# Memory rows, cached keys, spatial weights, conv taps, biases and norm weights are laid out feature-major by the host and loaded that way, in place of transposes on TensorE

## The chip, the cores and the metric

The kernel runs as one program on one core of a Trainium2 chip. The metric is the device time of one execution in microseconds (us). Five engines work in parallel, each through its own instructions in order: PE (TensorE, matmuls; its weight loads are shown apart as PEld), DVE (VectorE), ACT (ScalarE), POOL (GpSimd) and SP (SyncE, which here issues most of the loads). They wait for each other and for DMA through semaphores. SBUF is the on-chip memory, PSUM the memory that PE writes.

## What is computed

One layer of a decoder trunk for 256 prompt tokens and 8 sample tokens of one step each, in float32 with model width 2048. With `xn = rmsnorm(x)`:

```python
z = xn @ w_in                                  # 2048 x 9216, split into u, v, q, k, v, memory q, gates
o_g = gelu(zu) * (tril(ws) @ rmsnorm(gelu(zv)) + bs)      # 8 groups of a 128 x 128 matrix
o_a = sliding_window_attention(q, k, v, cached k and v of the samples)
o_m = attention(zm, memory k and v)             # 256 memory rows, 4 heads of 128
x = x + (sig(g0)*(o_g @ w_br_g) + sig(g1)*(o_a @ w_br_a) + sig(g2)*(o_m @ w_br_m)) @ w_out
h = rmsnorm(x) @ w_up                           # 2048 x 11264, then a causal conv of 3 taps + bias
x = x + (gelu(a) * b) @ w_down;  y = rmsnorm(x)
mkv = rmsnorm(mem_prompt) @ w_mem_kv            # 256 rows of 2048 -> 1024: memory k and v of the prompt
```

The conv's weights are `conv_w` (3 taps) and `conv_b` for 11264 channels, the spatial weights `gmlp_ws` and `gmlp_bs`, the norm weights four vectors of 2048, the cached keys 8 x 128 rows x 4 heads of 64. The host may lay inputs out anew before the launch; that is not in the time.

## The kernel before

**Matmuls.** Features lie on the partitions, tokens on the free axis. Each float32 product is made of three float32r matmuls: every operand is split into a high and a low part (`hi` a cast, `lo` the rest), and hi*hi, hi*lo and lo*hi are summed in PSUM. Weights come in **chunks** of 256 rows x 512 or 384 columns (512 or 384 KB). For each chunk SP issues one load into a tile `raw` (4 buffers), ACT casts its two halves to `whi`, DVE takes the rest to `wlo`, and PE runs the chunk's matmuls.

**What sets the order.** `run()` walks over all chunks. Before it emits the matmuls of a chunk it emits the load and the split of the chunk two further on. The class `InOrder` pins every engine to the order in which the code emits. All that is no weight work (norms, attention, transposes, stores, small loads) is put into numbered slots: `at(slot, fn)` and `later(n, fn)` keep a function for the n-th `pump()` from now, and the matmul code calls `pump()` once for every 128 output columns of a chunk (four times for a chunk of 512). So a small load stands on SP's queue between the weight loads of the chunks around it, and when its buffer isn't free, all loads behind it wait too.

**Stages.** The chunks are numbered from 0: q (0 to 15), k and v (16 to 23), memory q (24 to 31, `gemm` with `pre_m`), memory keys and values (32 to 47, `mem_chunk`), u and v of the gating branch (48 to 79), gates and branches, `w_out`, the conv feed-forward, and the final norm. Step k of the memory stage (k = 0 to 7) is chunks 32+2k (keys) and 33+2k (values). It needs rows 256k to 256k+255 of the memory's features: `mem_prep(k)` makes from them `mhi` (ACT) and `mlo` (DVE), two buffers each; it is called at the start of step k-1, behind the split of chunk 32+2k.

**What the change touches.** `mem_load` loads 512 columns of the memory rows for two steps as `ml` (2 buffers, 4 loads), `mem_prep` turns them with four transposes on PE into PSUM (`mtp`), and after the second step ACT takes squares of `ml` for the norm (`junk`, `ssm`). `swa_plan` loads the samples' cached keys as `k`, one per sample, turns each with two transposes (`ktrans`, `kctp`) and copies it to `KT` (`kcopy`, 4 buffers); `kscore` makes four samples' scores `ssp` from it, once for samples 0 to 3 and once for 4 to 7. `conv_plan` turns the taps (`crow`, `ctp`) into `cvT`, `gmlp_plan` the spatial weights (`wr`, `wtp`) into `wT` and the biases (`bsr`, `bstp`) into `bsT`. `gains` turns three norm weights (`grow`, `gtp`) and `x_start` the fourth (`gm`, `xgtp`) into `gT`.

Of the kernel before, what the change touches and what calls it, by code (L numbers as in the profile page):

```python
# [60 lines left out]
def body(ctx, tc, x_prompt, x_sample, cache_swa_k, cache_swa_v, cache_mem_k, cache_mem_v, state_conv,  # L61
         mem_prompt, norm_mix_g, w_in, gmlp_norm_g, gmlp_ws, gmlp_bs, attn_sinks, mem_norm_g, w_mem_kv,
         w_br_g, w_br_a, w_br_m, w_out, norm_ffn_g, w_up, conv_w, conv_b, w_down, final_norm_g,
         slope_col,
# [202 lines left out]

    def gains():
        tp = mis_t("gtp")
        T.transpose(out=tp[:, 0:48], in_=grow, identity=ident[:48, :48])  # L270
        V.tensor_copy(gT[:, 16:64], tp[:, 0:48])
# [1351 lines left out]
```

## Time and profile before

| | us |
|---|---|
| median of 3 runs | 1516.43 |
| lowest and highest of them | 1516.23, 1517.33 |
| the profiled execution | 1516.01 |
| its span in the trace | 1514.3 |
| PE busy | 1500.1 (99% of the span) |
| PEld, DVE, ACT, POOL busy | 1477.4, 1008.6, 766.3, 149.5 |

The page of the profile has the busy time of each engine, the span in 40 slices with the granted clock of TensorE and the traffic, and the chain of work that ended last. The trace behind it has every instruction with its start, its length, and the idle time before it with what ended that (in brackets). The profiled execution is 1.7 us longer than its span and 0.4 us shorter than the median. PE's records overlap, since matmuls are pipelined: what a matmul costs is the distance of two starts, not its length.

### The profile page before, as it was taken

Reading aid. Unit: us, or ns where it says so; the run is one execution under the profiler, and the core shown is the slowest. Engines: PE = TensorE matmul, PEld = TensorE weight load, DVE = VectorE, ACT = ScalarE, POOL = GpSimd, SP = SyncE. Lnnn points to the kernel's source line nnn. Section 1 sums busy time; section 2 is a strip of 40 time slices with the busy share of each in tenths; the row PEclk is TensorE's granted clock in tenths of the full one; section 3 lists DMA queues with packets and bytes.
Section 4 is the critical chain, followed back from the end, with each engine's and each line's share of the span. In section 5 each row is a group of like instructions: output and inputs, shape, how many; then the busy total and the mean of one; then the engine's idle time right before and its main releaser. Section 6 shows DMA issues by size and latency. Waiting matters only on the chain.

```text
span 1514.3 us, 31382 instructions
## 1 busy us (share of the span) xinstructions
PE 1500.1 (99%) x12091; PEld 1477.4 (98%) x12091; DVE 1008.6 (67%) x1918; ACT 766.3 (51%) x1473; POOL 149.5 (10%) x240
## 2 busy tenths in 40 slices
PE   9999999999999999999999999999999999999997
PEld 9987999999999999999999999999999999999997
DVE  6687797867564655755777777775445777777564
ACT  7477644456444444445555555554334555555443
POOL 0131251400000000001100000002000000000120
PEclk9999999999999999999999999999999999999999
DMA  7766797665565665555666666656556666665553
GB/s 236 200 195 178 222 326 245 217 208 177 181 180 176 183 178 182 179 183 179 180 180 182 180 182 181 181 182 188 181 181 181 181 181 181 181 178 184 178 166 114
DMA packets 155458, 285.83 MB, mean 189 GB/s; under 512 B 12340, under 2 KB 30708, under 8 KB 155300
## 3 DMA queue, kind: packets, MB, share of 16 engines
q1 hardware_dynamic: 151756, 276.23, 59.3%
q0 software_dynamic: 3376, 7.52, 1.9%
q8 instruction: 95, 1.56, 0.4%
q14 instruction: 55, 0.45, 0.1%
q10 hardware_dynamic: 176, 0.07, 0.0%
HBM read 279.36 MB, written 6.82 MB: 189 GB/s over the span
## 4 chain that ended last, share of the span: by engine, by line
PE 94%; DMA 2%; DVE 2%; ACT 1%; issue 1%; POOL 0%; POOLq 0%; DVEq 0%; SPq 0%; ACTq 0%
PE acc L50 87%; PE macc L50 3%; DMA raw<-in_w_in_dram 2%; DVE wlo L50 1%; ACT whi L50 0%; PE acc__182 L50 0%; PE acc__183 L50 0%; DMA sinkc<-in_attn_sinks_dram 0%; PE ov L50 0%; PE msov L50 0%; PE xtp L50 0%; PE sps L50 0%; PE wake L50 0%; PE ptp L50 0%; PE ytp L50 0%
## 5 line engine op out<-in xcount | busy, mean ns | idle before, releaser
L50 DVE TENSOR_TENSOR wlo<-raw,whi 128x512 fp32r<-128x512 f32 (+1 forms) x1008 | 657.6, 694 | 456.5 <-ACT whi L50 455.0
L50 ACT CAST whi<-raw 128x512 fp32r<-128x512 f32 (+1 forms) x1008 | 564.3, 608 | 590.3 <-PE acc L50 391.5
L50 PE MATMUL acc<-xg_hi,whi 128*128 128x264 f32 x1408 | 400.4, 284 | 0.0
L50 PE MATMUL acc<-xg_lo,whi 128*128 128x264 f32 x1408 | 400.3, 284 | 0.0
L50 PE MATMUL acc<-xg_hi,wlo 128*128 128x264 f32 x1408 | 400.2, 284 | 0.0
L50 PE MATMUL acc<-xhi,whi 128*128 128x264 f32 x1152 | 334.0, 291 | 0.4 <-ACT whi L50 0.2
L50 PE MATMUL acc<-xhi,wlo 128*128 128x264 f32 x1152 | 327.0, 284 | 0.3 <-DVE wlo L50 0.3
L50 PE MATMUL acc<-xlo,whi 128*128 128x264 f32 x1152 | 326.9, 284 | 0.0
L50 PEld LDWEIGHTS acc<-xg_hi,whi 128*128 128x128 f32 x1408 | 265.5, 189 | 0.0
L50 PEld LDWEIGHTS acc<-xg_lo,whi 128*128 128x128 f32 x1408 | 265.0, 188 | 0.0
L50 PEld LDWEIGHTS acc<-xg_hi,wlo 128*128 128x128 f32 x1408 | 264.5, 188 | 0.0
L50 PEld LDWEIGHTS acc<-xhi,whi 128*128 128x128 f32 x1152 | 217.0, 189 | 3.7 <-issue 1.7
L50 PEld LDWEIGHTS acc<-xlo,whi 128*128 128x128 f32 x1152 | 216.7, 188 | 0.6
L50 PEld LDWEIGHTS acc<-xhi,wlo 128*128 128x128 f32 x1152 | 216.1, 188 | 0.6 <-DVE wlo L50 0.5
L50 PE MATMUL acc<-ahi,whi 128*128 128x264 f32 x704 | 200.7, 285 | 0.0
L50 PE MATMUL acc<-ahi,wlo 128*128 128x264 f32 x704 | 200.1, 284 | 0.0
L50 PE MATMUL acc<-alo,whi 128*128 128x264 f32 x704 | 200.1, 284 | 0.0
L50 PEld LDWEIGHTS acc<-ahi,whi 128*128 128x128 f32 x704 | 132.7, 189 | 0.0
L50 PEld LDWEIGHTS acc<-alo,whi 128*128 128x128 f32 x704 | 132.6, 188 | 0.0
L50 PEld LDWEIGHTS acc<-ahi,wlo 128*128 128x128 f32 x704 | 132.2, 188 | 0.0
L50 DVE SCALAR_TENSOR_TENSOR t<-H,cvT,t 128x256 f32<-128x256 f32 x176 | 84.6, 481 | 3.1
L50 PE MATMUL acc<-mghi,whi 128*128 128x264 f32 x256 | 72.8, 284 | 0.0
(339 smaller groups left out, 1648.2 us busy)
## 6 DMA issues: line engine op xcount, KB each, us to landing
raw<-in_w_up_dram SPq DMA_DIRECT2D x176, 512.0 KB
raw<-in_w_in_dram SPq DMA_DIRECT2D x112, 512.0 KB
raw<-in_w_down_dram SPq DMA_DIRECT2D x88, 512.0 KB
raw<-in_w_in_dram SPq DMA_DIRECT2D x48, 384.0 KB
raw<-in_w_out_dram SPq DMA_DIRECT2D x32, 512.0 KB
raw<-in_w_mem_kv_dram SPq DMA_DIRECT2D x16, 512.0 KB
raw<-in_w_br_g_dram SPq DMA_DIRECT2D x12, 512.0 KB
raw<-in_w_br_a_dram SPq DMA_DIRECT2D x48, 128.0 KB
```

The source lines that it names most:

```text
L50: r = f(*a, **k)
```

## The change

Six inputs are laid out feature-major by the host and passed beside the others: `gains_t` (the four norm weights, 128 x 4 x 16), `taps_t` (128 x 4 x 88), `ws_t`, `bs_t`, `mem_t` (2048 x 256) and `key_t` (8 x 256 x 128). 63 transposes on PE go (32 `mtp`, 16 `kctp`, 8 `wtp`, 4 `ctp`, `gtp`, `bstp`, `xgtp`), with the copies of their results on ACT and DVE. `gT`, `cvT`, `wT`, `bsT` and `KT` are loaded; the causal mask is laid on `wT`, by POOL as before. The memory rows are loaded twice, as `mt` (feature-major, 8 loads of 256 KB, 3 buffers), from which `mhi` and `mlo` are made, and as `ml` (8 loads of 256 KB in place of 4 of 512 KB, 2 buffers) for the squares alone, which are taken after every step, 256 wide. `KT` has 6 buffers in place of 4, and its loads stand where `kload` is put in the plan. On ACT's queue `gT` is issued ahead of the sample rows `xs`.

```diff
-    gm = ld.tile([128, 128], F32, name="gm")
-    grow = ld.tile([48, 128], F32, name="grow")
...
+    gT = cst.tile([128, 64], F32, name="gT")
+    S.dma_start(gT, gains_t.rearrange("p r k -> p (r k)"))
     S.dma_start(xs, x_sample.rearrange("b o (k f) -> (b o k) f", f=128))
-    S.dma_start(gm[0:16, :], norm_mix_g[0].rearrange("(k p) -> k p", p=128))
...
-        if i == 7:
-            for j, g in enumerate((mem_norm_g[0], norm_ffn_g[0], final_norm_g)):
-                Y.dma_start(grow[16 * j:16 * j + 16, :], g.rearrange("(k p) -> k p", p=128))
...
-        T.transpose(out=tg[:, 0:128], in_=gm, identity=ident)
...
-        V.tensor_copy(gT[:, 0:16], tg[:, 0:16])
...
+    def mt_load(kc):
+        if kc < 8:
+            mt = M["mt", kc] = R["me"].tile([128, 2, 256], F32, name="mt", bufs=3)
+            Y.dma_start(mt, mem_t[256 * kc:256 * kc + 256, :].rearrange("(j p) t -> p j t", p=128))
+
     def mem_load(i):
-        if i < 4:
-            ml = M["ml", i] = R["me"].tile([128, 2, 512], F32, name="ml", tag="ml", bufs=2)
-            Y.dma_start(ml, mem_prompt[0, :, 512 * i:512 * i + 512].rearrange("(t p) f -> p t f", p=128))
+        if i < 8:
+            ml = M["ml", i] = R["me"].tile([128, 2, 256], F32, name="ml", tag="ml", bufs=2)
+            Y.dma_start(ml, mem_prompt[0, :, 256 * i:256 * i + 256].rearrange("(t p) f -> p t f", p=128))
 
     def mem_prep(kc):
 
         me = R["me"]
-        ml = M["ml", kc // 2][:, :, 256 * (kc % 2):256 * (kc % 2) + 256]
-        tp = mis_t("mtp")
-        for j in range(2):
-            for tb in range(2):
-                c = 256 * j + 128 * tb
-                T.transpose(out=tp[:, c:c + 128], in_=ml[:, tb, 128 * j:128 * j + 128], identity=ident)
+        tp = M.pop(("mt", kc)).rearrange("p j t -> p (j t)")
         mhi = me.tile([128, 2, 256], F32R, name="mhi", bufs=2)
         mlo = me.tile([128, 2, 256], F32R, name="mlo", bufs=2)
         g = [gT[:, 16 + 2 * kc + j:17 + 2 * kc + j] for j in range(2)]
             V.scalar_tensor_tensor(out=mlo[:, j, :], in0=tp[:, 256 * j:256 * j + 256], scalar=g[j], in1=mhi[:, j, :],
                                    op0=mul_, op1=sub_)
         M[kc] = (mhi, mlo)
-        if kc % 2:
-            junk = me.tile([128, 512], BF16, name="junk", bufs=1)
-            for tb in range(2):
-                later(3 + 2 * tb, lambda tb=tb: S.activation(junk, M["ml", kc // 2][:, tb, :], AF.Square,
-                                                             accum_out=ssm[:, tb, kc // 2:kc // 2 + 1]))
-            later(9, lambda: mem_load(kc // 2 + 2))
+        later(5, lambda: mt_load(kc + 3))
+        junk = me.tile([128, 256], BF16, name="junk", bufs=1)
+        for tb in range(2):
+            later(3 + tb, lambda tb=tb: S.activation(junk, M["ml", kc][:, tb, :], AF.Square,
+                                                     accum_out=ssm[:, tb, kc:kc + 1]))
+        later(6, lambda: mem_load(kc + 2))
 
     def pre_m(kc):
         if kc == 0:
             f4("qmT")
             R["me"] = st_me.enter_context(tc.tile_pool(name="me", bufs=1, side="right"))
+            for i in range(3):
+                mt_load(i)
             mem_load(0)
             mem_load(1)
...
+            Y.dma_start(cvT, taps_t)
...
-        def ktrans(b):
-            kt = B.pop(("k", b))
-            tp = B["tp", b] = mis_t("kctp")
-            for q in range(2):
-                T.transpose(out=tp[:, 128 * q:128 * q + 128], in_=kt[:, 128 * q:128 * q + 128], identity=ident)
-
-        def kcopy(b):
-            KT = B["KT", b] = st["s"].tile([128, 2, 129], F32, name="KT", bufs=4)
-            S.copy(KT[:, :, 0:128], B.pop(("tp", b))[:, 0:256].rearrange("p (a b) -> p a b", a=2))
-            V.tensor_copy(KT[:, :, 128:129], R["kvT"][:, 0:2, 256 + b:257 + b])
+        def kload(b):
+            KT = B["KT", b] = st["s"].tile([128, 2, 129], F32, name="KT", bufs=6)
+            Y.dma_start(KT[:, :, 0:128], key_t[b].rearrange("(q p) w -> p q w", p=128))
+
+        def kown(b):
+            V.tensor_copy(B["KT", b][:, :, 128:129], R["kvT"][:, 0:2, 256 + b:257 + b])
...
-            p(s + 1 + 2 * k, load, "k", cache_swa_k, k)
-            p(s + 10 + 3 * k, ktrans, k)
-            p(s + 12 + 3 * k, kcopy, k)
+            p(s + (1 + 3 * k if k < 6 else 20 + k), kload, k)
+            p(s + (9 + 2 * k if k < 6 else 28 + k), kown, k)
...
-            for c in range(2):
-                Y.dma_start(st["wr", c], gmlp_ws[0, 4 * c:4 * c + 4].rearrange("g t s -> t g s"))
-            Y.dma_start(st["bsr"], gmlp_bs[0])
+            Y.dma_start(st["wT"], ws_t)
+            Y.dma_start(st["bsT"], bs_t)
...
+            w = st["wT"][:, 4 * c:4 * c + 4, :]
+            G.affine_select(out=w, in_=w, pattern=[[0, 4], [1, 128]], compare_op=ALU.is_ge, fill=0.0,
+                            base=0, channel_multiplier=-1)
...
+    def turned(rows):
+
+        a = np.stack(rows).reshape(len(rows), -1, 128)
+        return np.ascontiguousarray(a.transpose(2, 0, 1))
+
...
+    add("mem_t", np.ascontiguousarray(inputs["mem_prompt"][0].T))
+    add("key_t", np.ascontiguousarray(inputs["cache_swa_k"][0].reshape(8, 128, 256).transpose(0, 2, 1)))
```

SP's queue in the memory stage (`raw` are chunks 35 to 41 before, in brackets what each load waits for; the number of a name is its buffer). Before:

```order
L50 DMA raw_1593<-in_w_mem_kv_dram 128x2x512 [waits DMAHW0_49,DVE_49]
L50 DMA raw_1640<-in_w_mem_kv_dram 128x2x512 [waits DMAHW1_49,DVE_49]
L50 DMA ml_1664<-in_mem_prompt_dram 128x2x512 [waits PE_49,Activation_49]
L50 DMA raw_1684<-in_w_mem_kv_dram 128x2x512 [waits DMAHW2_49,DVE_49]
L50 DMA raw_1717<-in_w_mem_kv_dram 128x2x512 [waits DMAHW3_49,DVE_49]
L50 DMA raw_1761<-in_w_mem_kv_dram 128x2x512 [waits DMAHW4_49,DVE_49]
L50 DMA raw_1798<-in_w_mem_kv_dram 128x2x512 [waits DMAHW5_49,DVE_49]
L50 DMA ml_1823<-in_mem_prompt_dram 128x2x512 [waits PE_49,Activation_49]
L50 DMA raw_1843<-in_w_mem_kv_dram 128x2x512 [waits DMAHW7_49,DVE_49]
```

And after the change, from chunk 35 on:

```order
L50 DMA raw_1566<-in_w_mem_kv_dram 128x2x512 [waits DMAHW5_49]
L50 DMA mt_1582<-in_mem_t_dram 128x2x256 [waits DVE_49]
L50 DMA ml_1588<-in_mem_prompt_dram 128x2x256 [waits Activation_49]
L50 DMA raw_1616<-in_w_mem_kv_dram 128x2x512 [waits DMAHW6_49]
L50 DMA raw_1656<-in_w_mem_kv_dram 128x2x512 [waits DMAHW7_49,DMAHW1_49]
L50 DMA mt_1672<-in_mem_t_dram 128x2x256 [waits DMAHW0_49,DVE_49]
L50 DMA ml_1677<-in_mem_prompt_dram 128x2x256 [waits Activation_49]
L50 DMA raw_1693<-in_w_mem_kv_dram 128x2x512 [waits DMAHW2_49]
L50 DMA raw_1733<-in_w_mem_kv_dram 128x2x512 [waits DMAHW3_49]
```

Before, one `ml` stood behind four chunks, with waits for PE and ACT (the readers of its buffer). Now `mt` and `ml` stand behind every two chunks: `mt` waits for DVE (`mlo` of three steps before has read its buffer) and `ml` for ACT (the squares).

ACT's queue at the same place, from `mhi` of step 3 on (`whi` are chunks 39 and 40, `pT` are attention's probabilities, `oa_hi` its output). Before:

```order
L50 ACTIVATE mhi_1732<-mtp_1727,gT_103 128x256 [waits PE_49]
L50 ACTIVATE mhi_1732<-mtp_1727,gT_103 128x256
L50 COPY pT0_1402<-ptp_1706 128x3x128
L50 ACTIVATE junk_1738,ssm_111<-ml_1053 128x512
L50 COPY pT1_1450<-ptp_1746 128x3x128 [waits PE_49]
L50 CAST whi_1763<-raw_1761 128x512 [waits DMAHW1_49]
L50 CAST whi_1764<-raw_1761 128x512 [waits PE_49]
L50 ACTIVATE junk_1738,ssm_111<-ml_1053 128x512 [waits Activation_49]
L50 CAST whi_1800<-raw_1798 128x512 [waits DMAHW2_49,PE_49]
L50 CAST whi_1801<-raw_1798 128x512 [waits PE_49]
L50 ACTIVATE mhi_1813<-mtp_1808,gT_103 128x256 [waits PE_49]
L50 ACTIVATE mhi_1813<-mtp_1808,gT_103 128x256
```

And now:

```order
L50 ACTIVATE mhi_1703<-mt_1417,gT_88 128x256 x2
L50 COPY pT0_1373<-ptp_1682 128x3x128
L50 ACTIVATE junk_1709,ssm_108<-ml_1588 128x256 [waits DMAHW5_49,Activation_49]
L50 COPY pT1_1425<-ptp_1717 128x3x128 [waits PE_49]
L50 ACTIVATE junk_1709,ssm_108<-ml_1588 128x256 [waits Activation_49]
L50 CAST whi_1735<-raw_1733 128x512 [waits DMAHW3_49]
L50 CAST whi_1736<-raw_1733 128x512 [waits PE_49]
L50 CAST whi_1775<-raw_1773 128x512 [waits DMAHW6_49,PE_49]
L50 CAST whi_1776<-raw_1773 128x512 [waits PE_49]
L50 ACTIVATE mhi_1783<-mt_1582,gT_88 128x256 [waits DMAHW4_49]
L50 ACTIVATE mhi_1783<-mt_1582,gT_88 128x256
```

The squares `junk` of a step now stand after `mhi` of every step; `mhi` is read from `mt`, so it waits for a DMA where it waited for PE.

SP's queue where the last two keys are loaded, in the u and v stage (`v` and `mkc` are cached values and memory keys of the samples, the last `raw` of the part is chunk 72). Before:

```order
L50 DMA raw_2970<-in_w_in_dram 128x2x384 [waits DMAHW5_49,DVE_49]
L50 DMA v_3003<-in_cache_swa_v_dram 128x256 [waits DMAHW6_49,PE_49]
L50 DMA raw_3017<-in_w_in_dram 128x2x384 [waits DMAHW7_49,DVE_49]
L50 DMA mkc_3033<-in_cache_mem_k_dram 128x512 [waits DMAHW0_49,Pool_49]
L50 DMA raw_3060<-in_w_in_dram 128x2x384 [waits DMAHW1_49,DVE_49]
```

And now:

```order
L50 DMA raw_2910<-in_w_in_dram 128x2x384 [waits DMAHW1_49,DVE_49]
L50 DMA v_2940<-in_cache_swa_v_dram 128x256 [waits DMAHW2_49]
L50 DMA raw_2951<-in_w_in_dram 128x2x384 [waits DMAHW3_49,DVE_49]
L50 DMA KT_2967<-in_key_t_dram 128x2x128 [waits DMAHW4_49,PE_49]
L50 DMA mkc_2969<-in_cache_mem_k_dram 128x512 [waits DMAHW5_49,Pool_49]
L50 DMA KT_2977<-in_key_t_dram 128x2x128 [waits DMAHW6_49,PE_49]
L50 DMA raw_2992<-in_w_in_dram 128x2x384 [waits DMAHW7_49,DVE_49]
```

Two `KT` loads that wait for PE (the scores `ssp` of samples 0 to 3, whose `KT` buffers they take) stand ahead of a weight chunk.

## Rows read from the trace of the kernel before

**Rows 1.** The page's chain that ended last, share of the span by engine.

```profile
PE 94%; DMA 2%; DVE 2%; ACT 1%; issue 1%; POOL 0%; POOLq 0%; DVEq 0%; SPq 0%; ACTq 0%
```

**Rows 2.** Windows (us; PE, PEld, DVE, ACT, POOL busy; PEclk, DMA share, GB/s): memory stage.

```profile
99.00:154.00 55.00, 54.86 (x271) 42.27 (x271) 41.72 (x101) 38.71 (x97) 14.97 (x28) 1.00 0.61 178
```

**Rows 3.** Timeline (start, length, engine, operation, idle before) of PE around one `mem_prep`.

```profile
112.68 0.39 PE L50 MATMUL macc<-whi,mlo 128*128 128x512 f32 x1
112.91 0.60 PE L50 MATMUL mtp<-ident,ml 128*128 128x128 f32 x4
...
113.58 0.40 PE L50 MATMUL macc<-wlo,mhi 128*128 128x512 f32 x1
```

**Rows 4.** Transposes by tile: count, shortest/median/longest ns, first and last start.

```profile
L50 PE MATMUL mtp<-ident,ml x32: 270/272/329, 88.5 to 141.7; 128*128 128x128 f32 x32
...
L50 PE MATMUL kctp<-ident,k x16: 270/272/276, 195.0 to 213.2; 128*128 128x128 f32 x16
...
L50 PE MATMUL wtp<-ident,wr x8: 271/272/273, 345.0 to 347.3; 128*128 128x128 f32 x8
...
L50 PE MATMUL ctp<-ident,crow x4: 240/241/243, 81.3 to 86.0; 88*128 88x88 f32 x4
```

**Rows 5.** Timeline of SP's queue from 80 to 120 us.

```profile
80.08 14.61 SPq L50 DMA_DIRECT2D raw<-in_w_mem_kv_dram  x5
104.91 0.37 SPq L50 DMA_DIRECT2D ml<-in_mem_prompt_dram  x1
105.37 3.81 SPq L50 DMA_DIRECT2D raw<-in_w_mem_kv_dram  x4
118.80 0.37 SPq L50 DMA_DIRECT2D ml<-in_mem_prompt_dram  x1
```

**Rows 6.** Timeline of ACT from 104 to 125 us.

```profile
104.17 0.63 ACT L50 ACTIVATE junk<-ml 128x512 bf16<-128x512 f32 x1
104.70 0.19 ACT L50 ACTIVATION_READ_ACCUMULATOR junk<-ml 128x1 f32 x1
...
111.09 1.14 ACT L50 CAST whi<-raw 128x512 fp32r<-128x512 f32 x2 [0.64 <-DMA raw<-in_w_mem_kv_dram]
...
113.81 1.12 ACT L50 CAST whi<-raw 128x512 fp32r<-128x512 f32 x2
114.84 0.83 ACT L50 ACTIVATE mhi<-mtp,gT 128x256 fp32r<-128x256 f32 x2
...
116.55 0.48 ACT L50 COPY pT<-ptp 128x384 f32<-128x384 f32 x1
...
124.38 1.25 ACT L50 CAST whi<-raw 128x512 fp32r<-128x512 f32 x2 [0.50 <-DMA raw<-in_w_mem_kv_dram]
```

**Rows 7.** Timeline of DVE from 102 to 117 us.

```profile
102.36 0.86 DVE L50 SCALAR_TENSOR_TENSOR mlo<-mtp,gT,mhi 128x256 fp32r<-128x256 f32 x2
...
115.81 0.86 DVE L50 SCALAR_TENSOR_TENSOR mlo<-mtp,gT,mhi 128x256 fp32r<-128x256 f32 x2
```

**Rows 8.** Timeline of PE: attention's output in step 2, third matmul of step 6.

```profile
118.67 2.16 PE L50 MATMUL ov<-pT,vv_tm 128*64 128x384 f32 x12
...
142.26 0.40 PE L50 MATMUL macc<-whi,mlo 128*128 128x512 f32 x1
```

**Rows 9.** Timeline of SP's queue: the load of chunk 72.

```profile
203.22 0.38 SPq L50 DMA_DIRECT2D raw<-in_w_in_dram  x1
```

**Rows 10.** Timeline of PE: scores of samples 0 to 3, first matmul of chunk 72.

```profile
207.79 0.65 PE L50 MATMUL ssp<-KT,QZ 128*32 128x129 f32 x16
...
215.51 0.29 PE L50 MATMUL acc<-xhi,whi 128*128 128x264 f32 x1
```

**Rows 11.** Windows, columns as in rows 2: around chunk 72, and the end.

```profile
210.00:220.00 10.00, 10.00 (x95) 9.66 (x93) 9.86 (x23) 4.93 (x13) 5.86 (x6) 1.00 0.97 333
1506.00:1510.00 4.00, 0.00 (x0) 0.00 (x0) 1.39 (x4) 0.93 (x2) 0.00 (x0) 0.69 0.92 319
1510.00:1515.00 5.00, 0.00 (x0) 0.00 (x0) 0.00 (x0) 0.00 (x0) 0.00 (x0) 0.50 0.52 178
```

More of the change, by code (lines that the diff above doesn't have):

```diff
@@ L176, in body @@
     pTs = cst.tile([128, 2, 32], F32, name="pTs")
-    ssm = cst.tile([128, 2, 4], F32, name="ssm")
+    ssm = cst.tile([128, 2, 8], F32, name="ssm")
     rmm = cst.tile([128, 2], F32, name="rmm")
@@ L220, in x_start @@
             T.matmul(wake[:, 0:128], lhsT=ones, rhs=ones, start=True, stop=True)
-        tx, tg, t0, t1 = mis_t("xstp"), side_t("xgtp"), mis_t("xtp"), side_t("xtp")
+        tx, t0, t1 = mis_t("xstp"), mis_t("xtp"), side_t("xtp")
         T.transpose(out=tx[:, 0:128], in_=xs, identity=ident)
         t0 = x_trans(t0[:, 0:256], 0, 0)
-        T.transpose(out=tg[:, 0:128], in_=gm, identity=ident)
         t1 = x_trans(t1[:, 0:256], 0, 1)
@@ L266, in q_norm @@
         V.tensor_tensor(q, q, r_bc.unsqueeze(1).to_broadcast([128, 3, NT]), op=mul_)
[L268 to L271, printed above, removed]
     items = []
@@ L426, in body @@
         at(slot, f)
-    at(62, gains)
     at(66, st_ld.close)
@@ L580, in opening @@
             s5 = st["p"] = st_s5.enter_context(tc.tile_pool(name="s5", bufs=1))
-            st["crow"] = []
-            for c in range(4):
-                crow = s5.tile([88, 128], F32, name="crow", bufs=4)
-                Y.dma_start(crow, (conv_w[0, c] if c < 3 else conv_b[0]).rearrange("(k p) -> k p", p=128))
-                st["crow"].append(crow)
+            Y.dma_start(cvT, taps_t)
             for c in range(2):
@@ L593, in load @@
                 G.dma_start(si[32 * q:32 * q + 16, :, :], sv[q][:, 22 * c:22 * c + 22, :])
-        def taps_(i):
-            tp = mis_t("ctp")
-            T.transpose(out=tp[:, 0:88], in_=st["crow"][i], identity=ident[:88, :88])
-            later(1, lambda: V.tensor_copy(cvT[:, i, :], tp[:, 0:88]))
         def rows(c, k):
@@ L619, in conv_plan @@
         p(b, opening)
-        for i in range(4):
-            p(b + 10 + 2 * i, taps_, i)
         for c in range(4):
@@ L1125, in opening @@
             s1 = st["p"] = st_s1.enter_context(tc.tile_pool(name="s1", bufs=1))
-            for n, sh in (("gbc", [128, 768]), ("bsr", [8, 128]), ("w00", [8, 8]), ("b00", [8, 8]),
+            for n, sh in (("gbc", [128, 768]), ("w00", [8, 8]), ("b00", [8, 8]),
                           ("wT", [128, 8, 128]), ("bsT", [128, 8]), ("vg", [128, 2, 768]), ("vs", [8, 768]),
@@ L1129, in opening @@
                 st[n] = s1.tile(sh, F32, name=n)
-            for c in range(2):
-                st["wr", c] = s1.tile([128, 4, 128], F32, name="wr%d" % c)
         def loads():
-            for c in range(2):
-                Y.dma_start(st["wr", c], gmlp_ws[0, 4 * c:4 * c + 4].rearrange("g t s -> t g s"))
-            Y.dma_start(st["bsr"], gmlp_bs[0])
+            Y.dma_start(st["wT"], ws_t)
+            Y.dma_start(st["bsT"], bs_t)
             Y.dma_start(st["gbc"], gmlp_norm_g[0].partition_broadcast(128))
@@ L1142, in causal @@
         def causal(c):
-            wr = st["wr", c]
-            G.affine_select(out=wr, in_=wr, pattern=[[0, 4], [-1, 128]], compare_op=ALU.is_ge, fill=0.0,
-                            base=0, channel_multiplier=1)
-        def w_trans(c):
-            tp = A["w", c] = mis_t("wtp")
-            for g in range(4):
-                T.transpose(out=tp[:, 128 * g:128 * g + 128], in_=st["wr", c][:, g, :], identity=ident)
-        def w_copy(c):
-            S.copy(st["wT"][:, 4 * c:4 * c + 4, :], A.pop(("w", c)).rearrange("p (g t) -> p g t", g=4))
-        def b_trans():
-            tp = A["b"] = mis_t("bstp")
-            T.transpose(out=tp[:, 0:8], in_=st["bsr"], identity=ident[:8, :8])
-        def b_copy():
-            V.tensor_copy(st["bsT"], A.pop("b")[:, 0:8])
+            w = st["wT"][:, 4 * c:4 * c + 4, :]
+            G.affine_select(out=w, in_=w, pattern=[[0, 4], [1, 128]], compare_op=ALU.is_ge, fill=0.0,
+                            base=0, channel_multiplier=-1)
         def rows(tb):
@@ L1616 @@
     add("slope_col", sc)
+    def turned(rows):
+        a = np.stack(rows).reshape(len(rows), -1, 128)
+        return np.ascontiguousarray(a.transpose(2, 0, 1))
+    add("gains_t", turned([inputs[n].reshape(-1) for n in ("norm_mix_g", "mem_norm_g", "norm_ffn_g", "final_norm_g")]))
+    add("taps_t", turned([*inputs["conv_w"][0], inputs["conv_b"][0]]))
+    add("ws_t", np.ascontiguousarray(inputs["gmlp_ws"][0].transpose(2, 0, 1)))
+    add("bs_t", np.ascontiguousarray(inputs["gmlp_bs"][0].T))
+    add("mem_t", np.ascontiguousarray(inputs["mem_prompt"][0].T))
+    add("key_t", np.ascontiguousarray(inputs["cache_swa_k"][0].reshape(8, 128, 256).transpose(0, 2, 1)))
     for i, shape in enumerate(_OUTS):
```

10 lines of the change are left out of this document (2 added, 8 removed).

## The prediction

> **What bounds the kernel now.** I read the chain that ended last first [rows 1]: 94% of it is PE, 2% DMA. The reader is to see that PE's instructions set the end, so a microsecond taken from PE is one won, as long as PE does not wait for it elsewhere. Then the windows of the memory stage, where most of the removed work lies [rows 2]: PE is busy 54.86 of 55 us there at the full granted clock (1.00, the 2.4 GHz level), DVE 41.72, ACT 38.71, the DMA engines 0.61. Nothing waits for data before the change; the stage has room on the other engines, but less than a third. After that I read what PE pays for a group of transposes, and last the queues that feed PE in two places where the change puts loads that wait in front of weights.
>
> **What is removed.** The matmul at 112.68 and the transposes behind it start 0.23 apart, which is what one such matmul costs; from the first of four `mtp` at 112.91 to 113.58 there are 0.67 us with one matmul in them (left out there), so the four cost 0.67 - 0.23 = 0.44 us [rows 3]. There are 32 `mtp` in 8 groups: 8 x 0.44 = 3.5. `kctp` and `wtp` have the same median length, 272 and 271 ns against 272 [rows 4], so I take 0.11 each: 16 x 0.11 = 1.76 and 8 x 0.11 = 0.88. The 4 `ctp` are narrower (241 ns): 4 x 0.11 = 0.44. `gtp` and `bstp` are small singles; between nothing and a full length of 0.27 I take 0.22 each, 0.45. Sum 3.5 + 1.76 + 0.88 + 0.44 + 0.45 = 7.0 us, all on the path, bounds 6.2 (without the singles and with 0.09 for each small one) and 7.4. The copies out of PSUM that go with them (ACT, DVE) are no part of the path.
>
> `xgtp` lies in the start, where PE is waiting anyway. There one load on ACT's queue replaces a load, a transpose and a copy, but the sample rows now stand second in the queue: I take nothing, with 0.4 either way (the length of one issue on SP's queue, 0.37 [rows 5]). The taps, the spatial weights and the biases are loaded once, long ahead of their use, behind weights that have buffers to spare there; their loads number fewer or equally many, so they cost nothing. Were that cover gone, one issue of 0.37 for each of the four loads would be late. The second copy of the memory rows is 2 MB more traffic: at 333 GB/s, the rate of the busiest window [rows 11], 6.3 us of DMA in a 55 us stage that uses 0.61 of its DMA time. By bytes it fits.
>
> **What is added: loads that wait, in front of weights.** Before, SP's queue stood once for `ml` in every four chunks: the row of five weight loads ends at 80.08 + 14.61 = 94.69, and the next thing is `ml` at 104.91, when the squares had been taken (104.70 + 0.19 = 104.89 [rows 5, 6]). Then four weight loads follow without a stop. Now there is a pair `mt`, `ml` in front of every two chunks, and both wait: `mt`(k+3) for `mlo`(k) and `ml`(k+2) for the squares of step k. Behind the pair stands the first weight chunk of step k+1, and on ACT and DVE `mhi`(k+1) and `mlo`(k+1) stand behind that chunk's split. So there is a loop: end of `mlo`(k) -> `mt`, `ml` issued -> weights of step k+1 land -> `whi` -> `mhi` -> `wlo`, `mlo`(k+1). It turns once per step, and no buffer shortens it.
>
> Its length, link by link. (1) From the end of `mlo` to the issue of `ml`: ACT takes in that time what stands between `mhi` and the last square, such as two `pT` of 0.48 and two squares of half of 0.63 + 0.19, 0.4 each, so 1.8 us after `mhi` [rows 6], and `mlo` ends 1.0 after `mhi` does (115.81 + 0.86 = 116.67 against 114.84 + 0.83 = 115.67 [rows 6, 7]). That leaves 0.8; between 0.5 (squares right behind `mhi`, as in step 1) and 1.4 (three more pieces of attention between) I take 1.0. (2) From the issue of `ml` to the first `whi` of the chunk behind it: 104.91 to 111.09 is 6.2, and 118.80 to 124.38 is 5.6, both with ACT shown waiting for that DMA [rows 5, 6]. `ml` has 256 KB less now, 0.8 us at 333 GB/s: 4.8 to 5.4. I take 5.0 since `mt` is partly in its way. (3) From that `whi` to the end of `mlo`: 113.81 to 116.67, 2.9 [rows 6, 7]. The loop takes 0.5 + 4.8 + 2.9 = 8.2 to 1.4 + 5.4 + 2.9 = 9.7 us; I take 8.8, and 8.3 for the first turn.
>
> What PE gives it: `mlo`(1) ends at 102.36 + 0.86 = 103.2 [rows 7], and PE wants `mlo`(6) for the third matmul of step 6, before at 142.26 [rows 8], and 6 x 0.44 = 2.6 earlier with the transposes gone: 139.7. (Step 6 is the last whose weights stand behind a pair.) So five turns have 36.5 us, 7.3 each. They take 8.3 + 4 x 8.8 = 43.5. **PE waits 7.0 us** in this stage, if the loop binds, with bounds of 5 x 8.2 = 41.0 (4.5) and 5 x 9.7 - 0.5 = 48.0 (11.5). The first of it should be seen in step 2, where PE's `ov` (118.67 before [rows 8]) needs `pT`, which ACT copies behind the split of chunk 38 and `mhi`(3): two turns after 103.2 less the split's own place, some 4 us late. What is late there hides nothing, since PE's next work, step 3, needs the same chunk.
>
> **The keys.** Loads for samples 6 and 7 wait for the scores of samples 0 to 3, which end at 207.79 + 0.65 = 208.4 [rows 10], and chunk 72, issued at 203.22 before [rows 9], stands as fourth behind them: 208.4 + 3 x 0.46 = 209.8 (the distance of two issues, 104.91 to 105.37 [rows 5]). From issue to `whi` it was 111.09 - 105.37 = 5.7 and 124.38 - 119.26 = 5.1 behind `ml` (119.26 is 0.46 after 118.80), less 0.4 for the smaller chunk: `whi` from 214.5 to 215.1, done 0.9 to 1.1 later, and PE wants it at 215.51 - 0.7 = 214.8 (three groups of keys are gone by then; the matmuls' own stall and gain cancel) [rows 6, 10]. Late by 0.6 to 1.4. DVE is busy 9.86 of 10 us there and the DMA engines 0.97 [rows 11], so chunk 73 can be late as well. I take 1.0 between 0 (the load comes as fast as without traffic) and 2.8 (both chunks at 1.4).
>
> **Sum.** -7.0 + 7.0 + 1.0 + 0 = +1.0 on the profiled execution's 1516.0, so 1517.0; the median of the runs stands 0.4 above that execution: **1517.4 us**.
>
> **Clock.** The trace shows the granted clock fall only at the end: with PE at 0 busy it is 0.69 in 1506 to 1510 and 0.50 (the 1.2 GHz level) in 1510 to 1515 [rows 11]. A wait of 4 us at `ov` would be the first such stop in mid-kernel. If a step of 24 matmuls behind it ran at 0.50, 24 x 0.23 = 5.6 us would be added, less what the loop would have PE wait anyway; I take 3 to 5.6. The Trainium skill, page "TensorE: Matmul & The Clock Gate", section "HAM oscillation — how this bites in real kernels", tells of a kernel in which waits for DMA between groups of matmuls let the clock drop, so that the next group began slow. By that rule the sum would be 1520.4 to 1523; by the rows before, which have no such wait, 1517.4. That rule speaks against the change, and no run so far can show it.
>
> **The rivals.** (a) *The loop doesn't bind*: the weights land faster than behind 512 KB of `ml`. With link 2 at 4.0 a turn is 0.9 + 4.0 + 2.9 = 7.8, five are 39.0, PE waits 2.5 or nothing, and the keys cost 0 to 1: 1516.4 - 7.0 + (0 to 3.5) = 1509.4 to 1513, middle 1511. For it: the DMA engines have 0.39 free in the stage, and each turn has one `ml` of half size. Against it: both landings that the trace shows in this place, 5.6 and 6.2, are long with the same share. (b) *Slower*: the same loop at its long end, squares late by 1.4, landing 5.4, DVE late with `wlo`. It decides from 9.1 a turn (8.6 + 4 x 9.25 = 45.6, a wait of 9.1, +3.1 in sum); at 9.7 the wait is 11.5 and the time 1516.4 - 7.0 + 11.5 + 1.0 = 1521.9. For it: ACT has exponentials of attention between `mhi` and the squares in steps 2 and 5. Against it: the shorter landing was the later one. (c) *The clock falls* in the wait at `ov`: 1520.4 to 1523, as above. That the transposes remain is none: the order of PE's instructions has none of these 63.
>
> **How the numbers follow.** A run of this kernel can tell about 0.2%, 3.0 us, from no change: faster is under 1513.4, slower over 1519.5. Forecast with a wait of 4.1 to 10 us: 0.48, same. Rival (a): 0.28, faster. Rival (b): 0.17 and (c): 0.07, slower, 0.24 together. The range that holds 8 in 10 runs from 1510.0, the lower part of (a), to 1522.0, the long end of (b); what is left out is the lowest of (a) and most of (c). The forecast's own range is 1513.4 to 1519.5.
>
> **What would show it.** Right: in 104 to 150, `mt` and `ml` on SP's queue start when `mlo` and the squares end; ACT sits idle before each first `whi` of a step until the DMA of `raw`; PE waits some 4 us at `ov` in step 2 and then at the start of steps 4 to 6; the window from 99 to 154 has PE busy clearly less than its length. From 350 on the two traces run alike but for 1.3 us (`wtp` and `bstp`, gone without a price). At chunk 72 PE waits for `whi` or `wlo` by about 1 us. Wrong: PE without waits in the memory stage; then link 2 was too long, and the time is near 1511. If the granted clock reads under 1.00 after `ov`, (c) has come. If waits appear in the start, or behind the loads of taps or spatial weights, what I costed at nothing was not.

## The result and the profile after

The changed kernel takes **1537.24 us** (median of 4 runs, 1536.31 to 1538.52) against 1516.33 before (1515.99 to 1517.33): ratio 1.0133, 95% interval 1.0121 to 1.0145. It is 20.9 us slower. The forecast was 1517.4, a loss of 1.0, and the range ended at 1522.0: the size of the loss was missed by far. The profiled execution has a span of 1536.0 us against 1514.3, so the trace holds the whole difference (21.7).

**Where the time went.** PE's weight matmuls are the same in both kernels, so the first matmul of each chunk can be found by counting them. This table is worked out so, in us from the first matmul of one chunk to that of another; the last row is from chunk 127 to the last matmul.

| stretch | before | after | what was removed there |
|---|---|---|---|
| start to chunk 0 | 6.7 | 7.9 | `xgtp` |
| 0 to 31 (q, k and v, memory q) | 88.9 | 87.5 | `gtp`, `ctp`, one group of `mtp` |
| 31 to 48 (memory stage) | 58.5 | 74.9 | seven groups of `mtp` |
| 48 to 60 (u, first of v) | 32.2 | 32.2 | nothing |
| 60 to 80 (rest of u and v, keys) | 47.7 | 54.8 | `kctp` |
| 80 to 127 (gates, gating branch) | 163.2 | 161.6 | `wtp`, `bstp` |
| 127 to the end | 1106.7 | 1106.7 | nothing |

Two stretches lose 16.4 and 7.1 us; the start loses 1.2 (e3 takes that up), and the others win or stay. The same two show in the windows of the trace after (columns as in [rows 2]):

```profile
99.00:154.00 55.00, 42.59 (x181) 30.70 (x181) 33.98 (x79) 31.79 (x90) 11.80 (x26) 0.92 0.55 170
154.00:232.00 78.00, 75.97 (x558) 69.80 (x559) 59.16 (x126) 42.57 (x104) 23.55 (x26) 0.97 0.74 231
232.00:330.00 98.00, 91.26 (x709) 87.07 (x710) 76.52 (x142) 45.13 (x102) 31.06 (x34) 0.97 0.74 235
```

PE, busy 54.86 of 55 us before [rows 2], is busy 42.59 now, at a mean granted clock of 0.92, and the DMA engines are less busy (0.55 against 0.61) with 2 MB more to move: they have been kept waiting too. The page's chain that ended last, as in [rows 1], has PE down by two points and DMA up by one:

```profile
PE 92%; DMA 3%; DVE 2%; ACT 1%; issue 1%; POOL 0%; SPq 0%; POOLq 0%; ACTq 0%; DVEq 0%
```

**Who PE waits for** is the view that decides. It lists the waiting tile, the engine and tile that ended the wait, the sum, the count and the longest. First from 90 to 160 us, then from 205 to 245:

```profile
PE ptp L50 <- DVE s L50: 5.8, 3, 3.9
PE macc L50 <- DVE qmT L50: 3.2, 1, 3.2
PE macc L50 <- ACT mhi L50: 2.8, 1, 2.8
PE ov L50 <- ACT pT L50: 0.7, 1, 0.7
PE ptp L50 <- ACT s L50: 0.6, 1, 0.6
```

```profile
PE acc L50 <- DVE vT L50: 5.0, 1, 5.0
PE acc L50 <- ACT whi L50: 1.7, 1, 1.7
```

Together 19.8 us. Only 4.5 of them are waits that the prediction's loop has: `whi` (1.7), made from the late weights, and `mhi` (2.8), which stands on ACT behind their cast. The other 15.3 are for attention's probabilities (`s`, `pT`) and for results that have to leave PSUM (`qmT`, `vT`): work that needs none of the late weights. Waits are not the whole price: while PE was busy at a granted clock of 0.50 it lost some 5.5 us more in the memory stage and 1.5 at the keys (half of that time, an estimate from the trace's record of the clock); e10 asks what that costs.

**How that comes about** is seen at step 0 of the memory stage. SP's queue (timeline: start, length, operation, count):

```profile
79.76 0.37 SPq L50 DMA_DIRECT2D raw<-in_w_mem_kv_dram  x1
90.92 0.37 SPq L50 DMA_DIRECT2D mt<-in_mem_t_dram  x1
91.64 0.37 SPq L50 DMA_DIRECT2D ml<-in_mem_prompt_dram  x1
92.06 2.31 SPq L50 DMA_DIRECT2D raw<-in_w_mem_kv_dram  x3
105.97 0.37 SPq L50 DMA_DIRECT2D mt<-in_mem_t_dram  x1
106.38 0.47 SPq L50 DMA_DIRECT2D ml<-in_mem_prompt_dram  x1
106.90 0.98 SPq L50 DMA_DIRECT2D raw<-in_w_mem_kv_dram  x2
115.35 0.37 SPq L50 DMA_DIRECT2D mt<-in_mem_t_dram  x1
116.56 0.37 SPq L50 DMA_DIRECT2D ml<-in_mem_prompt_dram  x1
```

Chunk 32 is issued at 79.76; chunk 33 only at 92.06, behind `mt`, which waited for `mlo`(0). Before, five weight loads left between 80.08 and 94.69 [rows 5]. DVE at the same place (the bracket is the idle time before an instruction and what ended it):

```profile
99.93 1.29 DVE L50 TENSOR_TENSOR wlo<-raw,whi 128x512 fp32r<-128x512 f32 x2 [3.44 <-ACT whi L50]
101.14 1.10 DVE L50 SCALAR_TENSOR_TENSOR qmT<-acc,r_bc 128x264 f32<-128x264 f32 x3
```

And PE:

```profile
101.71 0.77 PE L50 MATMUL macc<-whi,mhi 128*128 128x512 f32 x1 [3.21 <-DVE qmT L50]
102.28 0.63 PE L50 MATMUL macc<-wlo,mhi 128*128 128x512 f32 x1
```

`wlo` at 99.93 is the rest of chunk 33. It was emitted two chunks ahead, so on DVE it stands in front of `qmT`, the result that must leave PSUM before PE can begin step 0. DVE stood idle 3.44 us for chunk 33, `qmT` stood behind it though its inputs were there, and PE stopped in front of chunk 32, whose weights had been ready since 94 us. The last row shows the second effect: `macc` of 0.63 us against 0.39 in [rows 3]; from 102 to 106 the granted clock is 0.66, after PE had stood for 3.2 us. At chunk 72 it is the same with `vT` in the place of `qmT`: the two held `KT` loads leave at 223.34 and 224.43, chunk 73 lands late, its `wlo` starts at 235.41, and `vT` of the matmuls long done stands behind it. PE stops for 5.0 us at 232.90, in the middle of chunk 72.

### The profile page after: what moved, and what is told of

It is laid out like the page before. It is cut to its first block, busy times and chain, and to the rows that moved or that the text cites. A ratio compares the mean times of both kernels' runs of the same rounds, so it can differ in the third digit from the quotient of the medians.

```text
span 1536.0 us, 31232 instructions
## 1 busy us (share of the span) xinstructions
PE 1501.5 (98%) x12028; PEld 1476.2 (96%) x12028; DVE 1010.0 (66%) x1911; ACT 765.5 (50%) x1479; POOL 146.5 (10%) x239
## 4 chain that ended last, share of the span: by engine, by line
PE 92%; DMA 3%; DVE 2%; ACT 1%; issue 1%; POOL 0%; SPq 0%; POOLq 0%; ACTq 0%; DVEq 0%
PE acc L50 87%; DMA raw<-in_w_mem_kv_dram 2%; DVE wlo L50 1%; PE macc L50 1%; DMA raw<-in_w_in_dram 1%; PE acc__176 L50 0%; PE acc__177 L50 0%; ACT whi L50 0%; DMA xs<-in_x_sample_dram 0%; DMA si<-in_state_conv_dram 0%; PE xtp L50 0%; PE msov L50 0%; PE sps L50 0%; PE ytp L50 0%; PE mov L50 0%
## 5 line engine op out<-in xcount | busy, mean ns | idle before, releaser
L50 PE MATMUL acc<-mglo,whi 128*128 128x264 f32 x256 | 72.8, 284 | 0.0
```

The costliest lines, as they stand in the source:

```text
L50: r = f(*a, **k)
```

## Experiments

All are edits of the changed kernel, if nothing else is said, and compute all of it. The first matmul, the memory stage (chunk 31 to 48) and the keys' stretch (60 to 80) are read from each profiled execution as in the table above. The ratio is to runs of the kernel before on the same chip beside it (their medians were 1516.3 to 1516.9).

| kernel | time, us | ratio to before, 95% interval | first matmul | 31 to 48 | 60 to 80 |
|---|---|---|---|---|---|
| before | 1516.33 | | 6.7 | 58.5 | 47.7 |
| after | 1537.24 | 1.0133 [1.0121, 1.0145] | 7.9 | 74.9 | 54.8 |
| e1 `mt`, `ml` on ACT's queue | 1516.92 | 0.9998 [0.9988, 1.0008] | 6.7 | 55.2 | 54.5 |
| e2 keys unheld | 1534.5 | 1.0113 [1.0083, 1.0143] | 6.5 | 73.9 | 53.0 |
| e3 `xs` first | 1536.1 (one run) | | 7.1 | 75.0 | 53.9 |
| e4 e1, e2 and e3 | 1512.89 | 0.9972 [0.9963, 0.9982] | 6.5 | 55.1 | 49.6 |
| e5 only `mt` on ACT's queue | 1533.31 (one run) | | 6.5 | 71.5 | 55.1 |
| e6 only `ml` on ACT's queue | 1521.98 (one run) | | 6.3 | 61.6 | 53.5 |
| e8 e4 with the keys of before | 1512.12 | 0.9967 [0.9955, 0.9979] | 7.0 | 55.1 | 49.1 |
| e9 split one chunk later | 1516.01 | 0.9996 [0.9987, 1.0006] | 6.8 | 54.2 | 53.5 |
| e10 waits filled | 1536.35 | 1.0135 [1.0120, 1.0150] | 6.2 | 73.8 | 54.8 |
| e11 split later, e2 and e3 | 1510.59 | 0.9960 [0.9945, 0.9975] | 6.5 | 54.2 | 50.2 |
| e12 e11 and e1 | 1510.89 | 0.9966 [0.9956, 0.9976] | 6.5 | 54.2 | 50.8 |
| e13 before, split later | 1520.0 | 1.0018 [1.0009, 1.0028] | 7.3 | 58.1 | 52.2 |

### Holds or traffic: e1, e2, e3, e4

**e1** issues the memory rows from ACT's queue, where nobody's weights stand behind them:

```diff
-            Y.dma_start(mt, mem_t[...]...)
+            S.dma_start(mt, mem_t[...]...)
-            Y.dma_start(ml, mem_prompt[...]...)
+            S.dma_start(ml, mem_prompt[...]...)
```

> The changed kernel with the mt and ml loads issued from ACT's queue in place of SP's; nothing else differs. Theory H (held loads): what costs the time is that a load that waits for its buffer stands in front of weight loads on SP's queue. Then weights in the memory stage come as they came before, the waits of PE between 98 and 158 us (about 16.5 us net of the transposes saved) go, the 3 us of the transposes stay won: 1537.2 - 19.5 = about 1518. Theory T (traffic): the 2 MB more of memory rows and the smaller pieces fill the DMA engines, wherever they are issued: above 1530.

Measured 1516.92: theory H, traffic falls. The memory stage takes 55.2 us, 3.3 less than before: the seven groups of `mtp`. SP's queue has nothing but weights in it, and PE is busy in the whole window from 99 to 154 us, with the DMA engines more used there than before (0.74 against 0.61), so the 2 MB fit as the forecast said:

```profile
78.69 52.94 SPq L50 DMA_DIRECT2D raw<-in_w_mem_kv_dram  x16
```

```profile
99.00:154.00 55.00, 55.00 (x282) 43.42 (x279) 43.34 (x102) 42.76 (x116) 14.18 (x28) 1.00 0.74 218
```

The keys' wait stays (`PE acc` for `vT`, 5.6 us). Here a page and the run differ in what they make of it: the Trainium skill, page "DMA: Bandwidth & Descriptors", section "Issuing engines are not separate DMA queues", says that starting transfers from several engines saves only the time of issuing, which is small beside the transfer. By that, as an estimate from 16 issues of 0.37 us, e1 should be worth some 6 us at most; it is worth 20.3, because what is saved is the queue's standing, not its issuing.

**e2** gives the keys 8 buffers (two of the cached values take `KT` buffers that are free again, to make room):

```diff
-            KT = B["KT", b] = st["s"].tile([128, 2, 129], F32, name="KT", bufs=6)
+            KT = B["KT", b] = st["s"].tile([128, 2, 129], F32, name="KT", bufs=8)
```

> The changed kernel with 8 KT buffers in place of 6 (paid for by two of the cached values taking free KT buffers), so the loads of keys 6 and 7 wait for nobody; memory stage as changed. Theory H: the two waits of PE at chunks 72 and 73 (2.0 and 5.4 us, and the slow clock behind) go: 1537.2 - 8.9 = about 1528. Theory T: the DMA engines are full there (0.98) with or without the hold, the waits stay: above 1534.

Measured 1534.5. By the letter that is theory T (above 1534), but its four runs reach from 1529.53 to 1539.79 and decide little. In the profiled execution the stretch still takes 53.0 us with the hold gone, 5.3 more than before and hardly less than the 53.5 to 55.1 of the kernels that keep the hold, where H wanted 8.9 back. PE's waits from 180 to 250 us:

```profile
PE acc L50 <- DVE vT L50: 3.3, 1, 3.3
PE acc L50 <- DVE uT L50: 1.5, 1, 1.5
PE acc L50 <- DVE wlo L50: 0.3, 1, 0.3
```

So in this stretch the hold is only part of the loss; e8 takes it up. Why e4, with the same keys, takes 49.6 there and e2 doesn't, no run here shows. **e3** swaps the two loads on ACT's queue:

```diff
-    S.dma_start(gT, gains_t.rearrange("p r k -> p (r k)"))
     S.dma_start(xs, x_sample.rearrange("b o (k f) -> (b o k) f", f=128))
+    S.dma_start(gT, gains_t.rearrange("p r k -> p (r k)"))
```

> The changed kernel with the sample rows xs issued ahead of the norm weights gT on ACT's queue. If the 1.2 us lost in the start are the place of xs in the queue, the first weight matmul comes 1.2 us earlier, near 6.7 us, and the time is 1536. If gT is then the late one, the start stays as it is.

The first matmul comes at 7.1, not 6.7. But e1, e2 with gT first have it at 6.7 and 6.5, and e2's start is that of the changed kernel word for word. The 7.9 of the trace after was one execution's scatter (6.2 to 7.9 over all kernels here), and neither order of the two loads is shown to matter.

**e4** joins the three edits above.

> The three edits together (memory rows on ACT's queue, keys unheld, xs first). Theory H: nothing of the change's price is left and the 7 us of transposes are won: 1516.3 - 7 = 1509, at most 1511. Theory T: above 1525. If the slow clock were a cost of its own, it goes with the waits here and can't be told apart.

Measured 1512.89, profiled at 1510.33: faster than both kernels, but by 3.7 us in the median where H wanted 7. In the profiled execution, the fastest of the nine, what is missing lies between chunks 60 and 80; where the other 2.6 us of the median lie, no trace shows.

### Which of the two loads: e5, e6

e5 has only the first line of e1's edit, e6 only the second:

```diff
-            Y.dma_start(mt, mem_t[...]...)
+            S.dma_start(mt, mem_t[...]...)
```

> The changed kernel with only mt's loads moved to ACT's queue; ml stays on SP in front of the weights and waits for the squares of its step. Theory H says any load held in front of weights closes a loop: in the trace after the change a turn is squares end to ml 0.0, ml to the first whi 5.3 to 6.1, whi to the end of the squares 3.5, so 8.8 to 9.6; without mt's 256 KB ahead some 0.8 less, 8.0 to 8.8, still over the 7.3 that PE leaves: waits remain, about half go, 1528 to 1532. Theory M (mt alone is the hold): 1518.

```diff
-            Y.dma_start(ml, mem_prompt[...]...)
+            S.dma_start(ml, mem_prompt[...]...)
```

> The mirror: only ml's loads move to ACT's queue, mt stays on SP and waits for mlo. Theory H: a turn is mt to whi about 5.5 (1.2 less than now, since ml's wait no longer stands between) and whi to mlo's end 2.8, so 8.3 or a little less with 256 KB fewer ahead: waits remain, the one of 3.5 us at step 0 too, 1524 to 1530. Theory M: 1530 or more (only half of the bytes leave the queue). If ml alone were the hold: 1518.

Measured 1533.31 and 1521.98, one run each: either hold alone costs, as theory H said, and `ml`'s costs more (16.3 us over e1 in the memory stage against 6.4 for `mt`'s; both together 19.7). The turn of the loop is read from SP's `ml` in e5: 103.07, 112.05, 122.87, 132.50, 143.37, so 9.0 to 10.9 us; from `mt` in e6: 102.75, 111.09, 118.49, 127.12, so 7.4 to 8.6, around the 7.3 that PE leaves. `ml`'s release comes last, behind ACT's exponentials and squares, so it makes the longer loop; e6 came out 2 us better than expected, e5 1.3 worse.

### The order of ACT and DVE: e9, e10, e13

**e9** leaves loads and holds as they are, but emits the casts and rests of a chunk one chunk ahead of its use in place of two, in chunks 30 to 45 and 68 to 75 (the core of the edit; `raws` keeps the loaded chunks):

```diff
-                    ws[chunks[nxt]] = split(*items[chunks[nxt]][0])
+                    raws[nxt] = split_load(*items[chunks[nxt]][0])
                 nxt += 1
+                if 2 < nxt and not (30 <= pos < 46 or 68 <= pos < 76):
+                    while ns < nxt:
+                        ws[chunks[ns]] = split(*raws.pop(ns))
+                        ns += 1
...
+            while ns < nxt and ns <= pos + 1:
+                ws[chunks[ns]] = split(*raws.pop(ns))
+                ns += 1
```

> The changed kernel, loads and holds untouched, but in the memory stage and around the keys (positions 30 to 45 and 68 to 75 of the chunk list) the casts and rests (whi, wlo) are emitted one chunk ahead of their use in place of two. Theory Q (in-order queues): 15.3 of the 19.8 us that PE waits after the change are not for the late weights but for other work of ACT and DVE that stands behind their split (qmT and vT out of PSUM, s, pT); then these waits shrink, 1537 goes to 1525 or below. Theory W (weights themselves): PE needs the late chunk at the same time anyway, 1535 to 1540, or slower, since a split one chunk ahead has less slack.

Measured 1516.01: theory Q, far beyond its mark. The memory stage takes 54.2 us with every hold in its place, and PE waits for nothing there (a window as in [rows 2], then SP's queue):

```profile
99.00:154.00 55.00, 55.00 (x284) 43.90 (x284) 44.54 (x103) 46.42 (x125) 13.12 (x27) 1.00 0.78 238
```

```profile
101.62 0.37 SPq L50 DMA_DIRECT2D mt<-in_mem_t_dram  x1
102.37 0.37 SPq L50 DMA_DIRECT2D ml<-in_mem_prompt_dram  x1
...
108.00 0.37 SPq L50 DMA_DIRECT2D mt<-in_mem_t_dram  x1
108.70 0.37 SPq L50 DMA_DIRECT2D ml<-in_mem_prompt_dram  x1
...
114.65 0.37 SPq L50 DMA_DIRECT2D mt<-in_mem_t_dram  x1
```

The pairs still stand in front of the weights, but a turn takes 6.4 and 6.7 us where it took 9.4 (105.97 to 115.35). The late split does two things at once that this run can't part: `qmT`, `s` and `pT` no longer stand behind a chunk that hasn't landed, and `mhi`(k+1) stands behind the split of chunk 33+2k in place of 34+2k, the chunk that the hold delays, so the loop is cut. Both are the order of ACT and DVE. e1 takes the hold away and keeps the early split, e9 does the reverse, and either alone takes the loss out of the memory stage (55.2 and 54.2): it needs both. In the keys' stretch it helps little (53.5): there PE now waits 3.4 us for the held `KT` itself.

**e13** is the control: the kernel before with e9's edit, its range a little wider:

```diff
+                if 2 < nxt and not (30 <= pos < 46 or 62 <= pos < 78):
```

> Control: the kernel before the change with the same late split (chunks 30 to 45, 62 to 77). PE hardly waits in these stages before the change, so nothing is to be had: 1515.5 to 1517.5. If it comes below 1514, the late split is a gain by itself and what the other runs show is in part that.

Measured 1520.0, slower than expected. The memory stage is as fast as before or a little faster (58.1), so there the late split is free and no gain by itself worth the name; in the keys' stretch it costs 4.5 us, since DVE then is late with `wlo` (PE waits 1.7 us for it in three places, and 1.0 for a `whi`). What e9 wins in the memory stage is not a gain of the late split as such.

**e10** keeps PE busy through the six longest waits:

```diff
+    FILLT = {6: 5, 7: 17}
+
+    def fill(n):
+        f = mis_t("fill")
+        for _ in range(n):
+            T.matmul(f[:, 0:128], lhsT=ones, rhs=ones, start=True, stop=True)
...
+            if c == 0 and kc in (0, 5):
+                fill(14 if kc == 0 else 12)
...
+            if t in FILLT:
+                fill(FILLT[t])
...
+                    if kc == 0 and m < 2 and gap:
+                        fill((7, 22)[m])
```

> The changed kernel with small matmuls of ones on PE, whose result nobody reads, put in front of the six longest waits (14, 12, 5, 17, 7 and 22 of them at 0.213 us, some 2 us in all less than the waits). Theory C (the clock's fall after a wait is a cost of its own): the granted clock stays at 1.00, and 4 to 7 us of the time come back, 1530 to 1533. If the slow stretches only fill time in which PE would wait anyway: no change, 1536 to 1538; slower if the added matmuls run past the waits.

Measured 1536.35: no change that can be told (the intervals of the two ratios lie on each other). The windows around the waits, of the kernel after and then of e10:

```profile
98.00:106.00 8.00, 4.79 (x23) 3.32 (x22) 5.98 (x15) 5.59 (x14) 4.32 (x7) 0.79 0.38 98
142.00:150.00 8.00, 5.96 (x21) 4.43 (x21) 5.04 (x13) 5.71 (x20) 0.00 (x0) 0.79 0.39 125
230.00:246.00 16.00, 9.13 (x69) 8.14 (x69) 12.06 (x26) 5.89 (x16) 6.45 (x6) 0.79 0.81 262
```

```profile
98.00:106.00 8.00, 8.00 (x52) 6.51 (x52) 7.86 (x20) 6.59 (x19) 2.87 (x5) 1.00 0.45 91
142.00:150.00 8.00, 7.04 (x45) 6.08 (x44) 4.72 (x13) 5.40 (x19) 0.00 (x0) 1.00 0.42 124
230.00:246.00 16.00, 15.58 (x138) 14.79 (x138) 11.89 (x31) 6.72 (x18) 6.88 (x6) 1.00 0.85 283
```

The granted clock is 1.00 (2.4 GHz) in all three where it was 0.79. In the memory stage no time came back that can be told: 73.8 against the 74.9, 73.9 and 75.0 of the changed kernel, e2 and e3, which all have this stage alike. What PE does faster after a wait it waits at the next one (`ov` waits 2.1 us for `pT` where it waited 0.7), because the loop sets the pace, not PE. There the slow clock is real and is hardly a cost of its own; the fills in front of steps 0 and 5 ran on for some tenths of a us after what they covered, so up to some 2 us stay open. At chunk 72 e10 decides nothing, since its last fill ran far past the wait that it was to cover. PE, then DVE:

```profile
232.07 5.07 PE L50 MATMUL fill<-ones 128*128 128x128 f32 x44
236.90 0.37 PE L50 MATMUL acc<-xhi,whi 128*128 128x264 f32 x1
```

```profile
233.82 1.10 DVE L50 TENSOR_TENSOR vT<-acc,r_bc 128x264 f32<-128x264 f32 x3
```

The first of the three `vT` was out of PSUM near 234.2, and PE went on at 236.90: in this execution the wait would have been some 2.2 us, and the fill itself took 2.6 more. So the 54.8 of the keys' stretch holds a loss of e10's own, and what the clock costs there is not shown.

### What is left, and the best: e8, e11, e12

**e8** is e4 with the keys as they were before the change (loaded by rows, 16 transposes on PE):

```diff
-        def kload(b):
+        def ktrans(b):
...
-            p(s + (1 + 3 * k if k < 6 else 20 + k), kload, k)
-            p(s + (9 + 2 * k if k < 6 else 28 + k), kown, k)
+            p(s + 1 + 2 * k, load, "k", cache_swa_k, k)
+            p(s + 10 + 3 * k, ktrans, k)
+            p(s + 12 + 3 * k, kcopy, k)
```

> The run with all three edits, but the keys as before the change (loaded row by row, 16 transposes on PE, 4 KT buffers). It asks what the waits at chunks 64 and 72 are from that stay with unheld keys (2 us for uT and vT, 1.3 for KT). Theory K (the loads of turned keys, 512-byte runs in a stage with full DMA engines): the waits go, and 1.76 us of kctp come back: 1516.4 - 7.0 + 1.8 = 1511. Theory S (the stage is full for DVE and DMA anyway): 2 us of waits stay, 1513.

Measured 1512.12, and the stretch takes 49.1 against 49.6 in e4: within what the runs can tell, the same. Each theory has a part: with the old keys 1.4 us of loss remain against before (`uT` 0.6, `vT` 0.5: the stage is full), and the turned keys add about as much waiting as the 1.76 us of transposes that they save. Taking the keys off PE is worth nothing that can be told in this place (the medians are 1512.12 and 1512.89).

**e11** puts e13's late split, e2 and e3 together; **e12** adds e1 to that.

> The changed kernel with the split one chunk ahead in chunks 30 to 45 and 62 to 77 of the list, 8 KT buffers and xs first; mt and ml stay on SP's queue and still wait for their buffers. If the order of ACT and DVE is what makes a held load dear, nothing is lost here though the holds in the memory stage are all there: 1509 to 1511. If the holds have a price of their own, 1513 or more.

> The run before with mt and ml on ACT's queue too, so nothing is held and the split is late: 1509 to 1510. If it is slower than the one before, the issues on ACT's queue (16 of them) cost something.

Measured 1510.59 and 1510.89: the same, e12 0.9 over what was expected. e11 beats both kernels (6.3 us under the 1516.87 of before beside it), with `mt` and `ml` still held on SP's queue, and its memory stage takes 54.2 like e12's, so the hold there has no price of its own once nothing that PE wants stands behind it. Between chunks 60 and 80 it loses 2.5 us, in part the late split's own price there (e13), so a late split in the memory stage alone is the next thing to try; it wasn't tried.

## Why the prediction was wrong

**What was removed: right, a little low.** The stretches without waits are shorter by 1.4 (0 to 31), 3.3 (31 to 48 in e1), 1.8 (48 to 71) and 1.6 us (80 to 127), in sum 8.1 where 7.0 was forecast (80 to 127 alone reaches from 160.6 to 162.4 over the kernels with this change). For the seven groups of four 3.1 was forecast; they gave 3.3 in e1, which still waits 0.5 us for `qmT`, and 3.9 from e13 to e9, which both wait for nothing there: 0.56 a group in place of 0.44.

**Traffic and start costed at nothing: right.** e1 moves the same 2 MB with one wait of 0.5 us (for `qmT`) up to chunk 48. The start is 0 within its scatter.

**Where the holds are: right; that they make a loop: right.** `mt` waits for `mlo`, `ml` for the squares (SP waits 38.6 us for `mlo` and 9.6 for `junk` from 80 to 160 us), and ACT stands before the first `whi` of a step for the DMA, up to 5.07 us.

**Where the loop starts: wrong.** The working let it begin at `mlo`(1), at 103.2 as before. But the pair `mt`(3), `ml`(2) already stands in front of chunk 33; `mlo`(1) ended near 105.9, and PE had lost 3.2 us at step 0 by then. The pairs should have been counted in the listed order of SP's queue from the first on.

**Link 2: mis-sized.** From `ml`'s issue to the first `whi` it took 5.0 by the working; the trace after has 6.2 (106.38 to 112.58), 5.3, 6.1, 6.1, 5.6. The 256 KB that `ml` lost were taken off (0.8 us), and for the 256 KB that `mt` puts in their place the working put on 0.2 at most (5.0 over 4.8): 512 KB stand in front, as before. Link 1 was 0.4 to 1.2 (0.5 to 1.4 taken), link 3 2.7 (2.9 taken). The turn by `mt`'s issues was 9.4, 9.3 and 9.6, at the long end of 8.2 to 9.7.

**What PE waits for: the step that failed most.** The working asked when `mlo`(6) would be there and took that for PE's wait. On rival (b)'s longest turn that gives 11.5; the stage lost 19.7 (74.9 against 55.2). PE stopped where other work of ACT and DVE stood behind the late split: `qmT` 3.2, `s` 6.4, `pT` 0.7 of 13.1 us. The forecast had one such place in sight (`pT` in front of `ov`, said to be 4 us and 0.7 in fact) and did not draw the conclusion that every result of ACT and DVE between two splits is in the same place. e9 shows that this order is the cause by changing nothing else; how much of its gain is the shorter loop and how much the results freed from behind the split, it doesn't part.

**The keys: 1.0 forecast (0 to 2.8), 9.0 measured** (chunks 71 to 74: 7.5 before, 16.5 after). Chunk 72 was to be issued 1.4 us after the held loads come free; it came 1.6 after the first of them (223.34 to 224.90). The wait for it was 1.7, near the bound. The 5.0 us for `vT` behind `wlo` of chunk 73 were not in the list, for the same reason as `qmT`: the first chunk of a group of results needs PSUM that DVE empties only behind the split of the group's second chunk.

**Rivals.** (b) had the mechanism and a price 15 us too low. (c): the clock did fall in mid-kernel, as the Trainium skill's page "TensorE: Matmul & The Clock Gate", section "HAM oscillation — how this bites in real kernels", tells of waits between groups of matmuls, and the trace agrees with it (0.50 from 236 to 238 us, PE idle since 233.3). It did not fall at `ov`, where the forecast had it, but behind the longer waits. The 3 to 5.6 us that the forecast gave it as an addition were not to be had back from the memory stage in e10; at the keys that stays open. (a)'s time, 1509.4 to 1513, is what e4 and e11 reach once the loop binds no more.

## What to carry to other kernels

A load that waits for a buffer must not stand in a queue in front of loads that somebody needs soon; put it on a queue where nothing urgent stands behind it, or emit it so late that its buffer is free. When a transfer can come late, do not ask only when its consumer needs it: list everything that stands behind its first reader on that reader's in-order engine (here the splits on ACT and DVE), above all what empties PSUM, and take the earliest need in that list. A wider look-ahead is no shield: work for two chunks ahead, put in front of work for now, hands every delay on to now. A shorter one has its price too: where DVE had no slack it cost 4.5 us (e13).
